# Latent attention in six query tiles: rotated parts of four heads in one tile, score matmuls of 64 and 32 rows for two heads in turn

## The chip, the core and the metric

The kernel runs on one core of a Trainium2 chip (trn2). A core has five engines with queues of their own: PE (TensorE, matrix products), DVE (VectorE), ACT (ScalarE), POOL (GpSimd, which here mostly issues the weight loads) and SP (SyncE, which issues other transfers). Matmuls write to PSUM, eight banks of 128 partitions by 512 fp32 values. The metric is the device time of one execution in microseconds (us), the median of several runs.

## The reference, cut to what matters

The program is two transformer blocks of two layers each, one after the other, over 512 tokens and 1024 features, in fp32. The change concerns one branch of the second block, multi-head latent attention with eight heads:

```
q = (rms_norm(cq, q_norm) @ w_uq).reshape(b, s, 8, 64 + 32)        # cq: 384 wide
q_nope, q_pe = q[..., :64], q[..., 64:]
kv = (rms_norm(ckv, kv_norm) @ w_ukv).reshape(b, s, 8, 64 + 64)    # ckv: 256 wide
k_nope, v = kv[..., :64], kv[..., 64:]
q_pe = apply_rope(q_pe, cos, sin)      # 32 wide, per head
k_pe = apply_rope(kpe, cos, sin)       # 32 wide, one for all heads
sc = (q_nope . k_nope + q_pe . k_pe) * 96 ** -0.5                  # causal mask, softmax, then @ v
```

`apply_rope` turns the two halves of the 32 values: x1 cos - x2 sin and x2 cos + x1 sin. The scores of a head are thus a product over 64 plain features plus one over 32 rotated ones.

## The kernel before

Activations lie feature-major: a tile `s` is 128 features by 512 tokens. Every operand of a large product is kept as a high part h (fp32r) and a rest l, and a product is three matmuls (`mm3`: h.l, l.h, h.h). A weight tile of 128 features by 128 outputs against 512 tokens is thus three matmuls of 128x512.

All work is first recorded as a list of operations (`Plan.record`) and then put in order by a planner (`Plan.schedule`): each engine takes the operation that is due first among those whose inputs it reckons ready and for which a buffer is free (100 `s` tiles of SBUF, 8 `ps` banks). All instructions are issued from one line of `issue`, L649 in the profile (L645 in the changed kernel), so rows are told apart by tile names and shapes. `ps` is a PSUM bank, `s` any SBUF tile, `ident` the identity for transposes.

The second block's layer runs a feed-forward part, the mixer, and another feed-forward part. In the mixer `mla` does the latent attention. It is interleaved with eight pieces of other work (`filler(i)`: two output tiles of the input projection each, 48 matmuls of 128x512, with a recurrent unit or a gated convolution behind them on DVE and ACT), so that PE has something to do while a softmax runs.

In `mla` before, for each head:
- one query tile of 128 rows per head: 64 plain features, the 32 rotated ones and the same 32 with their halves swapped (the columns of w_uq are laid out so). It is 9 matmuls of 128x512 (`pq`); multiplied by one table `self.cs[u]` (ones, cosines, signed sines) it holds what the scores need.
- the key tile has 128 rows to match: 64 rows of k_nope and 64 rows in which the sums that make the rotated key stand twice (`ksum`, `K`; `kk` is filled per pair of heads).
- `attend`: the scores of query block i (128 queries, i = 0 to 3) against the 128(i+1) keys it may see, 3 matmuls over all 128 rows each, into four banks; then `softmax`, then per key block transposes and the product with the values.

The product with the values and `softmax` are the same in both kernels. The first block's attention has scores over 64 rows (`scores` and `ask`): there two heads lie in rows 0 to 63 and 64 to 127 of one tile, and their matmuls are issued in turn.

Of the kernel before, what the change touches and what calls it, by code (L numbers as in the profile page):

```python
# [60 lines left out]
def constants():  # L61
# [25 lines left out]
    for off in (64, 0):  # L87
        r = (p - off) % 128
        is_cos = r < 32
        is_sin = (r >= 32) & (r < 64)  # L90
        cols.append(trig(np.where(r < 64, f2, 0.0), np.where(is_sin, 0.0, 1.0),
                         np.where(is_sin, sg2, 1.0)))
    cols = np.concatenate(cols, 1)
# [57 lines left out]
def lay_out(inp, nl1=2, nl2=2):  # L151
# [37 lines left out]
    uq = []  # L189
    for h in range(8):  # L190
        nope = 96 * h + np.arange(64)
        pe = 96 * h + 64 + np.arange(32)
        uq += [nope, pe, pe[sw]] if h % 2 == 0 else [pe, pe[sw], nope]
    uq = np.concatenate(uq)
# [471 lines left out]
class Net:  # L666
# [230 lines left out]
    def setup(self):  # L897
# [8 lines left out]
        self.cols = self.fixed("cols", [128, 16])  # L906
# [33 lines left out]
    def body(self):  # L940
# [14 lines left out]
        if self.nl2:  # L955
            pf = self.positions(1)
            self.cs = [self.trig(2, pf), self.trig(3, pf)]
# [126 lines left out]
    def attend(self, q, k, rows, rng, nkb, V, vcols, scale, y, yrows, sink=None, mask=None, order=None, starts=(),  # L1084
               stacked=False):
# [3 lines left out]
        lo, hi = rows  # L1089
        S = []  # L1090
        for i in range(4):
            a, b = rng[i]
            w = 128 * (b - a)
            ps = self.ps()[:, :w]
            cols = slice(128 * i, 128 * i + 128)
            kc = slice(128 * a, 128 * b)
            self.mm3(ps, q[0][lo:hi, cols], q[1][lo:hi, cols], k[0][lo:hi, kc], k[1][lo:hi, kc], True, True)
            S.append(ps)
        P = self.softmax(S, scale, sink, mask)
        yield  # L1100
        full = self.ps()
        po = full[0:64]
        order = order or list(range(nkb))
        for n, kb in enumerate(order):
# [8 lines left out]
            if stacked:  # L1113
                mm = nc.tensor.matmul
                mm(full[:, q0:q1], V[kb][:, vcols], h, start=kb in starts, stop=False, skip_group_check=True)
                mm(po[:, q0:q1], V[kb][:, vcols.start:vcols.start + 64], l, start=False, stop=n == nkb - 1,
                   skip_group_check=True)
            else:
                vh, vl = V[0][kb], V[1][kb]
                self.mm3(po[:, q0:q1], vh[:, vcols], vl[:, vcols], h, l, kb in starts, n == nkb - 1,  # L1120
                         skip_group_check=True)
        y = y[yrows[0]:yrows[1]]
        nc.copy(y, po)
        if stacked:
            self.tt(y, full[64:128], ALU.add, out=y)
# [567 lines left out]
    def mla(self, l, z, bias, filler):  # L1693
# [14 lines left out]
        kz = self.stt(z[5][0:64], bias(5)[0:64], self.cs[1][0:64], ALU.add, ALU.mult, out=z[5][0:64])  # L1708
# [6 lines left out]
        K = []  # L1715
        for i in range(4):
            h, l_ = self.t(F32R), self.t(F32R)
            rows = slice(64, 128) if i % 2 == 0 else slice(0, 64)
            self.split(pk[rows], h[rows], l_[rows])
            K.append((h, l_))  # L1720
# [21 lines left out]
        for p in range(4):  # L1742
# [3 lines left out]
            kk = [K[2 * (p % 2)], K[2 * (p % 2) + 1]]  # L1746
            for u in range(2):
                rows = slice(64 * u, 64 * u + 64)
                self.split(ps[rows], kk[u][0][rows], kk[u][1][rows])
            y = self.t()  # L1750
            for u in range(2):
                pq = self.ps()
                wh, wl = self.wsmall(I[f"b_uq{l}"][p][:, 3 * u:3 * u + 3])
                for k in range(3):
                    self.mm3(pq, wh[:, k], wl[:, k], cq[k][0], cq[k][1], k == 0, k == 2)
# [6 lines left out]
                for _ in g:  # L1762
                    pass
# [26 lines left out]
```

## Time and profile before

| | |
|---|---|
| median of 3 runs | 3475.35 us (3474.81 to 3476.16) |
| the profiled execution | 3479.35 us, span of its instructions 3477.6 us |
| PE busy | 3419.1 us, 98% of the span, 16304 matmuls |
| DVE busy | 1916.5 us, 55% |
| ACT, POOL busy | 888.7 us, 1748.9 us |
| granted TensorE clock, mean | 0.992 of full speed |

The span is the time from the first to the last instruction; the execution's own time is 1.75 us longer. Busy time is the union over an engine's instructions. Matmuls overlap in the records (each lasts longer than the distance to the next), so the price of a matmul is the distance between starts, not its own duration.

### The profile page before, as it was taken

The page shows a single profiled execution, that of the slowest core. Times are in us where ns is not written, and L with a number is a line of the kernel's source. Part 1 is how long each engine was busy: PE and PEld are TensorE (multiplying, and loading weights), DVE is VectorE, ACT ScalarE, POOL GpSimd, SP SyncE. Part 2 cuts the span into 40 slices and gives each one's busy share as a digit, 9 for nine tenths or more (in the row PEclk, how much of TensorE's full clock was granted, in tenths as well). Part 3 has the DMA queues.
Part 4 walks back from the last instruction along what each step waited for, and adds up shares of the span by engine and source line. Part 5 has one row for each costly group of instructions (what it writes and reads, how often), then busy time and mean ns, then how long its engine had stood idle before and what let it go on. Part 6 is the DMA issues. An engine that isn't in the chain of part 4 may idle for free.

```text
span 3477.6 us, 44658 instructions
## 1 busy us (share of the span) xinstructions
PE 3419.1 (98%) x16304; PEld 2853.3 (82%) x16304; DVE 1916.5 (55%) x3920; ACT 888.7 (26%) x1723; POOL 1748.9 (50%) x2433
## 2 busy tenths in 40 slices
PE   7999999999999999999999999999999999999998
PEld 5888888788888988888888888888888888888887
DVE  7863424766332733259996534244423999744332
ACT  4740002553000300026723200010001573421000
POOL 3454464354455644653456544654465336654462
PEclk9999999999999999999999999999999999999999
DMA  7788897698789887985899977998899669998794
GB/s 195 150 193 171 163 210 159 134 191 178 156 176 203 207 180 163 236 207 105 174 198 247 216 157 154 222 209 192 159 226 212 126 131 222 231 238 158 158 203 103
DMA packets 360444, 635.93 MB, mean 183 GB/s; under 512 B 40608, under 2 KB 63904, under 8 KB 360224
## 3 DMA queue, kind: packets, MB, share of 16 engines
q0 software_dynamic: 346752, 612.56, 82.7%
q1 hardware_dynamic: 13472, 20.52, 1.9%
q8 instruction: 128, 2.10, 0.2%
q14 instruction: 92, 0.75, 0.1%
HBM read 624.00 MB, written 6.29 MB: 181 GB/s over the span
## 4 chain that ended last, share of the span: by engine, by line
PE 90%; DVE 5%; DMA 2%; issue 1%; ACT 1%; POOL 1%; SPq 0%; DVEq 0%; POOLq 0%; ACTq 0%
PE ps L649 90%; DVE s L649 5%; ACT s L649 1%; DMA s<-in_b_in 1%; DMA s<-in_a_in 1%; POOL s L649 0%; DMA s<-s 0%; SPq L649 0%; DMA s<-in_b_mo 0%; DVE mx L649 0%; DVE sp L649 0%; POOL rinv L649 0%; ACT L649 0%; DVE rc L649 0%; ACT es L649 0%
## 5 line engine op out<-in xcount | busy, mean ns | idle before, releaser
L649 PE MATMUL ps<-s 128*128 128x512 f32 (+4 forms) x15706 | 3363.4, 376 | 42.4 <-DVE s L649 23.7
L649 PEld LDWEIGHTS ps<-s 128*128 128x128 f32 (+2 forms) x15706 | 2780.1, 188 | 592.5 <-ACT s L649 19.2
L649 POOL DMA_DIRECT2D s<-in_b x1088 | 786.4, 1034 | 666.3 <-DVE s L649 307.1
L649 ACT ACTIVATE s<-s 128x512 fp32r<-128x512 f32 (+2 forms) x696 | 393.6, 600 | 1721.1 <-DVE s L649 1133.6
L649 DVE TENSOR_TENSOR s<-ps,s 128x512 f32<-128x512 f32 (+5 forms) x634 | 394.2, 639 | 604.5 <-PE ps L649 601.3
L649 DVE TENSOR_SCALAR s<-s 128x512 fp32r<-128x512 f32 (+2 forms) x851 | 343.7, 423 | 449.7 <-DMA s<-in_b 246.3
L649 POOL DMA_DIRECT2D s<-in_a_f x544 | 397.4, 1037 | 355.0 <-DVE s L649 186.8
L649 DVE TENSOR_TENSOR s<-s 128x512 f32<-128x512 f32 (+3 forms) x812 | 493.0, 625 | 61.9 <-ACT s L649 35.4
L649 POOL DMA_DIRECT2D s<-in_b_in x368 | 290.4, 1017 | 265.5 <-ACT s L649 76.6
L649 DVE SCALAR_TENSOR_TENSOR s<-s,vecs 128x256 fp32r<-128x256 f32 (+22 forms) x438 | 284.1, 684 | 6.4 <-ACT s L649 3.4
L649 ACT ACTIVATE s<-s,vecs 128x512 f32<-128x512 f32 (+2 forms) x209 | 133.8, 661 | 305.6 <-DVE s L649 292.7
L649 DVE SCALAR_TENSOR_TENSOR s<-ps,s 128x512 f32<-128x512 f32 (+1 forms) x33 | 22.3, 675 | 200.0 <-PE ps L649 200.0
L649 ACT ACT_TABLE_LOAD x68 | 87.2, 1283 | 33.3 <-DVE s L649 31.5
L649 ACT ACTIVATE s<-ps 128x512 f32<-128x512 f32 (+1 forms) x40 | 21.4, 534 | 272.8 <-PE ps L649 237.3
L649 POOL DMA_DIRECT2D s<-in_a_in x64 | 47.6, 876 | 83.8 <-ACT s L649 27.4
L649 DVE CAST s<-s 128x512 fp32r<-128x512 f32 (+3 forms) x198 | 83.4, 422 | 5.4
L649 POOL DMA_DIRECT2D s<-in_a_out x64 | 46.5, 1064 | 63.5 <-PE ps L649 23.2
L649 ACT ACTIVATE s<-s,nb 128x256 f32<-128x256 f32 (+3 forms) x128 | 70.7, 555 | 27.1 <-DVE nb L649 27.0
L649 DVE RECIPROCAL s<-s 128x128 f32<-128x128 f32 (+1 forms) x45 | 73.1, 1635 | 7.4 <-ACT s L649 7.4
L649 POOL TENSOR_TENSOR rinv<-rms,nhalf 128x2 f32<-128x2 f32 (+1 forms) x19 | 18.6, 1029 | 98.4 <-DVE rms L649 96.5
L649 POOL DMA_DIRECT2D s<-in_b_out x64 | 48.6, 893 | 34.3 <-DVE s L649 16.2
L649 ACT CAST s<-ps 128x256 fp32r<-128x256 f32 (+4 forms) x131 | 55.9, 464 | 23.7 <-PE ps L649 18.7
(80 smaller groups left out, 905.0 us busy)
## 6 DMA issues: line engine op xcount, KB each, us to landing
s<-in_b POOLq DMA_DIRECT2D x1024, 256.0 KB, 6.4
s<-in_a_f POOLq DMA_DIRECT2D x512, 256.0 KB, 5.9
s<-in_b_in POOLq DMA_DIRECT2D x368, 256.0 KB, 6.3
s<-in_a_in POOLq DMA_DIRECT2D x64, 256.0 KB, 7.6
s<-in_a_out POOLq DMA_DIRECT2D x64, 256.0 KB, 6.5
s<-in_b_out POOLq DMA_DIRECT2D x64, 256.0 KB, 7.4
s<-in_b POOLq DMA_DIRECT2D x64, 128.0 KB, 6.3
s<-in_b_mo POOLq DMA_DIRECT2D x32, 256.0 KB, 6.3
```

Of the source, the lines that this page charges most:

```text
L649: getattr(getattr(nc, op.eng), op.fn)(*[real(v) for v in op.args], **{k: real(v) for k, v in op.kw.items()})
```

## The change

The query features are laid out as eight times 64 plain features (four tiles, one per pair of heads) and then eight times 32 rotated ones (two tiles, four heads each): six tiles, not eight.

```diff
-    uq = []
-    for h in range(8):
...
-        uq += [nope, pe, pe[sw]] if h % 2 == 0 else [pe, pe[sw], nope]
-    uq = np.concatenate(uq)
+    uq = np.concatenate([96 * h + np.arange(64) for h in range(8)] + [96 * h + 64 + np.arange(32) for h in range(8)])
...
-            self.cs = [self.trig(2, pf), self.trig(3, pf)]
+            self.cs = [self.trig(2, pf), self.trig(3, pf), self.trig(4, pf)]
```

The rotated tiles are made at the start of `mla` for all heads. The swap of the halves is done by eight transfers of 16 rows each, issued on SP, from a copy of the PSUM bank:

```diff
+        kp = self.split_t(pk)
...
+        qp = []
+        for t in range(2):
+            ps = query(4 + t)
+            raw, b = self.t(), self.t()
+            nc.copy(raw, ps)
+            for g in range(8):
+                nc.sync.dma_start(out=b[16 * g:16 * g + 16], in_=raw[16 * (g ^ 1):16 * (g ^ 1) + 16])
+            y = self.tt(ps, self.cs[1])
+            self.tt(b, self.cs[2], out=b)
+            qp.append(self.split_t(self.tt(y, b, ALU.add, out=y)))
```

The scores of two heads (u = 0, 1) are made together. For each query block, first the plain part from 64 rows (rows 0 to 63 and 64 to 127), then the rotated part from 32 rows (rows 0 and 32 on, or 64 and 96 on), accumulated in the same bank. A pair holds six banks; blocks 0 and 2 of a head share one.

```diff
+        def scores(p, qn, kn):
+            mm = nc.tensor.matmul
+            banks = [[self.ps() for _ in range(3)] for _ in range(2)]
+            S = [[b[0][:, 0:128], b[1][:, 0:256], b[0][:, 128:512], b[2]] for b in banks]
+            for i in range(4):
+                cols, kc = slice(128 * i, 128 * i + 128), slice(0, 128 * i + 128)
+                for part, (q, k) in enumerate(((qn, kn), (qp[p // 2], kp))):
+                    for n, (x, y) in enumerate(((0, 1), (1, 0), (0, 0))):
+                        for u in range(2):
+                            r = slice(64 * u, 64 * u + 64) if part == 0 else \
+                                slice(32 * (2 * (p % 2) + u), 32 * (2 * (p % 2) + u) + 32)
+                            mm(S[u][i], q[x][r, cols], k[y][r, kc], start=part == 0 and n == 0,
+                               stop=part == 1 and n == 2, skip_group_check=True,
+                               **(dict(tile_position=(r.start, 0)) if part else {}))
+            return S
...
+        heads = pair(0)
+        filler(0)
+        for p in range(4):
+            P = [self.softmax(t, 96 ** -0.5, mask=mask) for t in scores(p, *heads)]
...
+                if h + 1 < 8:
+                    filler(h + 1)
+                if u and p < 3:
+                    heads = pair(p + 1)
+                self.weigh(P[u], rng, 4, V[p // 2], ...)
```

`pair(p)` makes the plain key and query tiles of two heads (6 and 9 matmuls of 128x512, each split once over 128 rows); `weigh` is the second half of `attend`, unchanged.

What this does to the order of instructions is shown at three places. The first is PE in the second block's first layer, the scores of one head before (the second head of the first pair; `ps_14456` to `ps_14463` are its four banks, `s_14448` and `s_14452` its query, the other two its key):

```order
L649 MATMUL ps_14456<-s_14321,s_14448 128x128
L649 MATMUL ps_14458<-s_14321,s_14448 128x256
L649 MATMUL ps_14460<-s_14321,s_14448 128x384
L649 MATMUL ps_14463<-s_14321,s_14448 128x512
L649 MATMUL ps_14456<-s_14308,s_14452 128x128
L649 MATMUL ps_14456<-s_14308,s_14448 128x128
L649 MATMUL ps_14458<-s_14308,s_14452 128x256
L649 MATMUL ps_14458<-s_14308,s_14448 128x256
L649 MATMUL ps_14460<-s_14308,s_14452 128x384
L649 MATMUL ps_14460<-s_14308,s_14448 128x384
L649 MATMUL ps_14463<-s_14308,s_14452 128x512
L649 MATMUL ps_14463<-s_14308,s_14448 128x512
```

These twelve are all of a head's score matmuls, all over 128 rows, and they follow each other. In the changed kernel, PE at the start of the second pair of heads (`ps_14801` and `ps_14803` are the first banks of the two heads; `s_14717` and `s_14711` with `s_14771` and `s_14789` the 64-row parts of keys and queries, `s_14319`, `s_14329` with `s_14458`, `s_14462` the 32-row ones):

```order
L645 MATMUL ps_14801<-s_14717,s_14771 128x128
L645 MATMUL ps_14803<-s_14717,s_14771 128x128
L645 MATMUL ps_14801<-s_14711,s_14789 128x128
L645 MATMUL ps_14803<-s_14711,s_14789 128x128
L645 MATMUL ps_14801<-s_14711,s_14771 128x128
L645 MATMUL ps_14803<-s_14711,s_14771 128x128
L645 MATMUL ps_14801<-s_14329,s_14458 128x128
L645 MATMUL ps_14803<-s_14329,s_14458 128x128
L645 MATMUL ps_14801<-s_14319,s_14462 128x128
L645 MATMUL ps_14803<-s_14319,s_14462 128x128
L645 MATMUL ps_14801<-s_14319,s_14458 128x128
L645 MATMUL ps_14803<-s_14319,s_14458 128x128
```

One query block of two heads is six matmuls of 64 rows and then six of 32 rows, the two heads in turn; the same twelve follow with 256 and 384 columns. The second place is PE at the last query block (512 columns) of that pair, where `ps_14850` and `ps_14865` are the third banks of the two heads and `ps_14759` is a tile of the filler:

```order
L645 MATMUL ps_14850<-s_14717,s_14771 128x512
L645 MATMUL ps_14850<-s_14711,s_14789 128x512
L645 MATMUL ps_14850<-s_14711,s_14771 128x512
L645 MATMUL ps_14850<-s_14329,s_14458 128x512
L645 MATMUL ps_14850<-s_14319,s_14462 128x512
L645 MATMUL ps_14850<-s_14319,s_14458 128x512
L645 MATMUL ps_14759<-s_13575,s_13961 128x512
L645 MATMUL ps_14865<-s_14717,s_14771 128x512
L645 MATMUL ps_14865<-s_14711,s_14789 128x512
L645 MATMUL ps_14865<-s_14711,s_14771 128x512
L645 MATMUL ps_14865<-s_14329,s_14458 128x512
```

Here the two heads do not alternate: the planner found no bank for the second head in time, and its six matmuls come after the first head's six, with a 128-row matmul of the filler between. The third place is SP's queue in the second block's first layer, of the changed kernel:

```order
L645 DMA s<-in_pos 128x512
L645 DMA x<-s 128x512 x8
L645 DMA s<-in_c_ksum 64x128
L645 DMA s<-s 16x512 x16
L645 DMA s<-in_c_mask 128x512
L645 DMA s<-x 128x512 x8
```

The row `s<-s 16x512 x16` is new; before, `s<-in_c_mask` followed `s<-in_c_ksum` at once. It stands once in each of the two layers.

## Rows read from the trace of the kernel before

**Rows 1.** The page: busy time of the engines, granted clock in 40 slices.

```profile
PE 3419.1 (98%) x16304; PEld 2853.3 (82%) x16304; DVE 1916.5 (55%) x3920; ACT 888.7 (26%) x1723; POOL 1748.9 (50%) x2433
PEclk9999999999999999999999999999999999999999
```

**Rows 2.** Windows: feed-forward part, then the latent attention of both layers; columns in the header.

```profile
core 0: us, PE busy (x) PEld busy (x) DVE busy (x) ACT busy (x) POOL busy (x), PEclk, DMA share, GB/s
1200.00:1400.00 200.00, 200.00 (x884) 165.59 (x883) 82.36 (x155) 21.42 (x36) 100.58 (x138) 1.00 0.85 176
1560.00:1740.00 180.00, 177.34 (x860) 145.64 (x859) 171.64 (x373) 126.16 (x236) 72.82 (x102) 1.00 0.68 139
2715.00:2900.00 185.00, 183.18 (x885) 150.31 (x884) 177.53 (x382) 127.44 (x237) 76.98 (x107) 1.00 0.70 141
```

**Rows 3.** Waits of PE in 1560 to 1740: us in total, times, longest.

```profile
PE ps L649 <- DVE s L649: 2.2, 3, 1.5
PE ps L649 <- ACT s L649: 0.4, 1, 0.4
```

**Rows 4.** Timeline of PE: a head's first score matmul, and the matmul after its twelve.

```profile
start us, us, engine line op out<-in xcount [idle before <-releaser]
1583.35 0.22 PE L649 MATMUL ps<-s 128*128 128x128 f32 x1
1585.27 0.39 PE L649 MATMUL ps<-s 128*128 128x512 f32 x1
```

**Rows 5.** Timeline of PE round the first block's 64-row scores (rows*columns of the weights).

```profile
670.25 0.34 PE L649 MATMUL ps<-s 128*64 128x384 f32 x1
670.52 0.39 PE L649 MATMUL ps<-s 64*128 64x256 f32 x2
670.75 0.28 PE L649 MATMUL ps<-s 64*128 64x256 f32 x2
670.98 0.35 PE L649 MATMUL ps<-s 64*128 64x384 f32 x2
...
672.02 0.29 PE L649 MATMUL ps<-s 64*128 64x256 f32 x2
672.25 0.29 PE L649 MATMUL ps<-s 64*128 64x256 f32 x2
672.47 0.50 PE L649 MATMUL ps<-s 128*128 128x512 f32 x1
672.81 0.40 PE L649 MATMUL ps<-s 128*128 128x512 f32 x1
```

**Rows 6.** Groups of PE by shape within that burst, 670.60 to 672.30.

```profile
L649 PE MATMUL ps<-s 64*128 64x384 f32 x12 | 1.2, 332 | 0.0
L649 PE MATMUL ps<-s 64*128 64x256 f32 x12 | 1.1, 293 | 0.0
```

**Rows 7.** Timeline of PE's weight loads at the start of that burst.

```profile
670.52 0.19 PEld L649 LDWEIGHTS ps<-s 64*128 64x128 f32 x2 [0.30 <-issue]
```

**Rows 8.** Groups by shape, whole span: copies and rests of the key halves.

```profile
L649 DVE TENSOR_TENSOR s<-ps,s 64x512 fp32r<-64x512 f32 x24 | 16.5, 686 | 0.5
L649 ACT CAST s<-ps 64x512 fp32r<-64x512 f32 x16 | 9.2, 578 | 5.4 <-DVE s L649 3.1 <-PE ps L649 1.9
L649 DVE CAST s<-ps 64x512 fp32r<-64x512 f32 x8 | 5.5, 688 | 0.2
```

**Rows 9.** SP's transfers from tile to tile: ns per issue (min/median/max), and landing.

```profile
L649 SPq DMA_DIRECT2D s<-s x40: 507/590/832, 28.4 to 635.0; - x40
DMA to landing us min/median/max: 1.9/5.7/11.8
```

**Rows 10.** Windows in the first block: a stretch after PE waited, and one with 64-row scores.

```profile
648.00:654.00 6.00, 0.69 (x3) 0.54 (x3) 5.72 (x18) 1.76 (x6) 0.85 (x1) 0.50 0.22 34
666.00:672.00 6.00, 6.00 (x47) 5.10 (x47) 5.75 (x17) 4.68 (x12) 0.00 (x0) 1.00 0.00 1
```

More of the change, by code (lines that the diff above doesn't have):

```diff
@@ L1082, in softmax, with weigh @@
         return P
-    def attend(self, q, k, rows, rng, nkb, V, vcols, scale, y, yrows, sink=None, mask=None, order=None, starts=(),
-               stacked=False):
+    def weigh(self, P, rng, nkb, V, vcols, y, yrows):
         nc = self.nc
[L1089 to L1100, printed above, removed]
         full = self.ps()
         po = full[0:64]
-        order = order or list(range(nkb))
-        for n, kb in enumerate(order):
+        mm = nc.tensor.matmul
+        for kb in range(nkb):
             qs = [i for i in range(4) if rng[i][0] <= kb < rng[i][1]]
@@ L1112, in attend @@
             self.split(pt, h, l)
[L1113 to L1121, printed above, removed]
+            mm(full[:, q0:q1], V[kb][:, vcols], h, start=kb == 0, stop=False, skip_group_check=True)
+            mm(po[:, q0:q1], V[kb][:, vcols.start:vcols.start + 64], l, start=False, stop=kb == nkb - 1,
+               skip_group_check=True)
         y = y[yrows[0]:yrows[1]]
         nc.copy(y, po)
-        if stacked:
-            self.tt(y, full[64:128], ALU.add, out=y)
+        self.tt(y, full[64:128], ALU.add, out=y)
     def scores(self, heads, rng):
@@ L1714, in mla, with query @@
         nc.tensor.matmul(pk, ksum, kz, start=True, stop=True)
[L1715 to L1720, printed above, removed]
+        kp = self.split_t(pk)
+        qw = {}
+        def query(m):
+            if m // 2 not in qw:
+                qw[m // 2] = self.wload(I[f"b_uq{l}"][m // 2])
+            wh, wl = qw[m // 2]
+            ps = self.ps()
+            for k in range(3):
+                self.mm3(ps, wh[:, 3 * (m % 2) + k], wl[:, 3 * (m % 2) + k], cq[k][0], cq[k][1], k == 0, k == 2)
+            return ps
+        qp = []
[8 more added lines that the diff above has]
+            qp.append(self.split_t(self.tt(y, b, ALU.add, out=y)))
         uv = [self.wsmall(I[f"b_uv{l}"][:, 4 * i:4 * i + 4]) for i in range(2)]
@@ L1741, in mla, with pair @@
         yb = []
-        for p in range(4):
+        def scores(p, qn, kn):
+            mm = nc.tensor.matmul
+            banks = [[self.ps() for _ in range(3)] for _ in range(2)]
[11 more added lines that the diff above has]
+            return S
+        def pair(p):
             ps = self.ps()
```

28 lines of the change are left out of this document (8 added, 20 removed).

## The prediction

> **What bounds the kernel now.** I read the page first, then windows, then waits, then single matmuls. The page has PE busy for 98% of the span at full granted clock [rows 1]; the other engines have slack on the whole. A busy PE could still be a PE that idles in small pieces, so the pace was taken next: in a feed-forward stretch 884 matmuls of 128x512 take 200.00 us, 0.226 us each, and PE never stops [rows 2]. In the stretch where the change acts, latent attention, DVE is the second busiest, 171.64 of 180 us, and PE still runs for 177.34 [rows 2]. All that PE waits for there is 2.6 us in the first layer [rows 3]. So the time of this stretch is the number of PE slots times their price, and work taken from DVE or ACT can give back at most those waits. The sum is a PE sum.
>
> **Queries.** Eight tiles become six: 2 x 9 matmuls of 128x512 fewer in each of two layers, 36 x 0.226 = 8.1 us less. They stand in PE's queue with no wait behind them, so all of it is on the path.
>
> **Scores, if everything ran in pairs.** Before, a head's twelve score matmuls run from 1583.35 to 1585.27, 1.92 us [rows 4]; sixteen heads in two layers are 30.7 us. After, each of these is split in a 64-row and a 32-row one, 384 matmuls for 192. What two such matmuls of different heads cost is read from the first block, where 64-row matmuls of two heads are issued in turn. Each row of the timeline there holds two matmuls, so the two start together; from one such pair to the next, with 256 columns, it is (670.98 - 670.75)/2 = 0.115 us, and with 384 columns (672.02 - 670.98)/6 = 0.173 us [rows 5], for 24 matmuls in all [rows 6]. The pair costs what one matmul costs: 0.173 is 0.226 times 384/512 and a little. Taking the same for 32 rows, two heads need 2 parts x 12 slots where they needed 2 x 12 before: no gain and no loss.
>
> **Scores that have lost their partner.** The order of the changed kernel does not always alternate the heads. A pair wants six banks of eight, and at the last query block the second head often gets its bank too late, so its matmuls come behind the first head's. Over both layers 64 matmuls of 512 columns, 14 of 128 and 2 of 256 have no partner of the same size beside them. Two of these take two slots where a pair takes one: 32 x 0.226 + 7 x 0.12 + 0.12 = 8.2 us more. (A 128-column slot is what is left of a head's 1.92 us: 1.92/3 - 0.226 - 0.173 - 0.115 = 0.126.) This already eats the gain from the queries.
>
> **Changes of row height.** The first block also shows what it costs to go from 128-row to 64-row matmuls. The last of 128 rows starts at 670.25, the first 64-row pair at 670.52, the second at 670.75 [rows 5]: 0.50 us where the slots alone are 0.173 + 0.115 = 0.29. On the way back, 672.25, 672.47, 672.81 [rows 5]: 0.56 where 0.115 + 0.226 = 0.34 were due. So 0.2 us each way. The cause is visible: the weight load, which otherwise runs under the matmul before it, starts only at 670.52, after PE's load port idled for 0.30 us with nothing to wait for but issue, and the matmul has to sit through it (0.39 against 0.28 us) [rows 5, 7]. In the changed order the row height changes 45 times in the first layer's latent attention and 46 times in the second's, against 2 and 2 before (one 64-row product that makes the rotated key): 87 more. 30 of them are between 128 rows and 64 or 32; their price is the one read. The other 57 are between 64 and 32 rows, which nothing in this trace shows. Their bounds are nothing (both are parts of the array, and pairs at rows 0 and 64 do run together [rows 5]) and 0.2 us each. I take 0.2: a 32-row load goes to rows that the 64-row matmul before it is using, as a 64-row load goes to rows that a 128-row one is using, and that is the row that it is nearest to. 87 x 0.197 = 17.1 us.
>
> The Trainium skill, "TensorEngine Tiling (Array Packing)", Key Properties, says the same and against this change: switching the tiling mode, not just the tile, drains the engine. By it all 57 are paid and the sum is as below; without it they would be free and the sum 11.2 us lower. The trace agrees for 128 to 64 rows (0.2 us), and no run so far shows 64 to 32. "TensorE: Matmul & The Clock Gate", Part 3, has matmuls in different row groups run at once, 32-row ones too; the trace agrees for 64 rows.
>
> **What lies beside.** DVE and ACT lose the key halves, 24 copies and 24 rests of about 0.69 us [rows 8]; with the other splits and table products, 28 such DVE operations per layer become 17, 11 x 0.69 = 7.6 us. That is worth at most the 2.6 us of waits [rows 3], and I book nothing, since the new order makes waits of its own that I can't price. If DVE's relief were not there nothing would be lost either. The third table is made once, ahead of feed-forward work in which DVE is busy for less than half [rows 2]. The swap of the rotated halves: a copy, eight issues of 0.59 us, a landing of 5.7 us, then four DVE operations [rows 9, 8]: 0.6 + 4.7 + 5.7 + 2.8 = 13.8 us. In the new order 101 matmuls stand between the end of the query tile and its first use, of which 88 of 512 columns, some 22 us; PE does not wait. DVE waits in order: in its queue the product with the swapped tile stands behind some 39 operations that belong to other work, so it is not early at its wait. SP's queue has the sixteen transfers between two loads that are due later. Uncovered, the swap would cost the 13.8 us once per layer. Weight loads get fewer (twelve query loads per layer for sixteen), on a queue that PE does not wait for.
>
> **The sum.** -8.1 (queries) + 0 (paired scores) + 8.2 (unpaired ones) + 17.1 (row height) = +17.2 us. The profiled execution took 3479.35 us, span 3477.6; it would be 3496.5. It lies 4.0 us over the median of the runs, 3475.35, so the median comes to 3492.5.
>
> **The rivals.** A measurement of this kernel tells a change of 0.2%, 7.0 us, from none; "same" is 3468.4 to 3482.3.
> - *Free inner changes, not slower.* If PE lets a 32-row load run under a 64-row matmul, the 57 cost nothing: -8.1 + 8.2 + 30 x 0.197 = +6.0, 3481.3, inside the 0.2%. It decides from a price under 0.02 us each. For it: two 64-row tiles don't disturb each other [rows 5]. Against: the same rows are in use. 0.10.
> - *Half price.* Drain or load is hidden, not both: 57 x 0.1 less, 3486.8. For it: 0.2 us is two pieces, an idle port and a load [rows 7]. 0.10.
> - *Late swap or new waits.* Landings of 11.8 us [rows 9] and a DVE that is busy for 95% [rows 2] could use up the 8 us of slack; DVE, which works in order, then holds softmax and splits for PE. It costs once the chain passes 22 us, and 6 us per layer would give 3504.5. Against: PE waits for so little now [rows 3]. 0.06.
> - *32-row matmuls don't pair.* Then the rotated part of sixteen heads takes 30.7 us alone where the order's slots are 18.2: +12.5, 3505. For it: no row has 32 rows. 0.04.
> - *The clock.* In a stretch in which PE stood idle for 5.3 of 6 us the granted clock was 0.50, the lower of its two levels (1.2 of 2.4 GHz) [rows 10]; in one with 64-row scores it was 1.00 [rows 10], and the gaps here are 0.2 us. It is in the rest, with a gain that I don't see: 0.03.
>
> **How the numbers follow.** The sum as it stands has 0.67, between 3488 and 3498 (a wait of some us per layer more or less). The rivals have the rest. The likeliest case gives 3492.5. The range from 3481 to 3501 takes in the two cheaper prices of the inner changes and leaves out the late swap, the unpaired 32 rows and the rest, 0.13, with the tails. Faster by over 0.2% would need free changes and pairs where the order has none: 0.02. Within 0.2%: the free inner changes and little else, 0.12. Slower: 0.86.
>
> **What would show it.** In the profile after: groups of 32-row matmuls, two to a start; at each change from 64 to 32 rows a start that comes 0.2 us late, with the load not ahead of its matmul; 512-column score matmuls of one head alone, 0.226 us apart; 18 query matmuls fewer per layer; PE's waits in latent attention still 1 to 5 us. I am wrong if 64 to 32 follows without a gap (then 3481), if one change costs much more than 0.2 us, or if DVE's wait for the swapped tile ends with PE standing still.

## The result and the profile after

The changed kernel takes 3514.76 us, median of four runs (3509.11 to 3520.03), the kernel before 3475.08 in runs beside it (3474.64 to 3476.16): a ratio of 1.011, 95% interval 1.0098 to 1.0123, 39.7 us slower. The prediction was 3492.5, range 3481 to 3501. The sign was right and the size was not: about 22 us are missing in the sum.

The profiled execution took 3520.03 us, span 3518.3. Where the 40.7 us of span lie is found by the matmuls: PE works in program order, so the same matmul of the feed-forward parts can be found in both traces by counting, with 78 more per latent attention in the changed kernel (16460 records for 16304). Before the first latent attention it is 2.6 us later (the variants below are 0.3 to 3.9 us earlier there; nothing was changed in that part, so this is scatter), behind it 24.1, behind the second 41.1. So the first layer's mixer loses 21.5 us, the second's 16.9, and the long feed-forward parts nothing. The page's line of busy times, which answers to [rows 1]:

```profile
PE 3448.2 (98%) x16460; PEld 2860.3 (81%) x16460; DVE 1918.3 (55%) x3923; ACT 860.1 (24%) x1683; POOL 1744.2 (50%) x2425
```

PE is again "busy" for 98%: this number hides all of it. The windows that answer to [rows 2], two of the norm stages, which [rows 2] left out, and the burst (the score matmuls of one pair of heads, one behind the other) of the second pair in four pieces; columns as in [rows 2]:

```profile
1200.00:1400.00 200.00, 200.00 (x884) 165.62 (x883) 84.15 (x160) 22.68 (x37) 97.31 (x134) 1.00 0.84 176
1565.00:1760.00 195.00, 192.09 (x923) 148.73 (x922) 166.38 (x364) 111.72 (x216) 73.00 (x99) 0.95 0.63 130
2745.00:2930.00 185.00, 181.15 (x917) 142.79 (x917) 163.87 (x365) 111.17 (x214) 70.37 (x95) 0.99 0.65 131
...
1547.20:1562.00 14.80, 13.12 (x51) 9.35 (x50) 13.47 (x29) 7.08 (x13) 7.90 (x11) 0.88 0.85 211
2725.10:2742.10 17.00, 12.52 (x48) 8.75 (x48) 13.15 (x27) 6.74 (x13) 8.73 (x13) 0.80 0.91 238
...
1614.00:1620.00 6.00, 6.00 (x39) 4.87 (x38) 5.76 (x13) 4.46 (x9) 2.63 (x3) 1.00 0.63 94
1620.00:1626.00 6.00, 6.00 (x42) 3.53 (x40) 5.87 (x13) 1.19 (x1) 0.84 (x1) 0.88 0.46 75
1626.00:1632.00 6.00, 6.00 (x14) 3.92 (x14) 5.13 (x17) 4.81 (x12) 2.49 (x4) 0.50 0.53 95
1632.00:1638.00 6.00, 6.00 (x22) 4.79 (x21) 2.54 (x8) 1.99 (x5) 0.00 (x0) 0.77 0.30 90
```

The first line agrees with [rows 2] to the matmul. The others show two things that [rows 2] did not have. The granted clock is 0.95 and 0.99 in the scores, where it was 1.00: (1 - 0.95) x 195 + (1 - 0.99) x 185 = 11.6 us. In the burst it falls to 0.50, the lower of its two levels (1.2 of 2.4 GHz), while PE is busy for 6.00 of 6.00 us and never waits; 14 matmuls then take the time of 26. And the norm stages hold few matmuls: 51 records in 14.80 us, 48 in 17.00.

The burst that begins all this is dense only to the eye. Starts of its matmuls, two to a row, which answer to [rows 5]; the last line is the weight load, as in [rows 7]:

```profile
1620.85 0.28 PE L645 MATMUL ps<-s 64*128 64x256 f32 x2
1620.97 0.28 PE L645 MATMUL ps<-s 64*128 64x256 f32 x2
1621.17 0.38 PE L645 MATMUL ps<-s 32*128 32x256 f32 x2
1621.40 0.28 PE L645 MATMUL ps<-s 32*128 32x256 f32 x2
1621.52 0.28 PE L645 MATMUL ps<-s 32*128 32x256 f32 x2
1621.73 0.44 PE L645 MATMUL ps<-s 64*128 64x384 f32 x2
1622.01 0.33 PE L645 MATMUL ps<-s 64*128 64x384 f32 x2
...
1621.17 0.18 PEld L645 LDWEIGHTS ps<-s 32*128 32x128 f32 x2
```

From 64 to 32 rows: 1621.40 - 1620.97 = 0.43 us where two slots of 0.117 were due, 0.20 more. From 32 to 64: 1622.01 - 1621.52 = 0.49 for 0.117 + 0.173, again 0.20. The load starts with its matmul and not ahead of it. Two 32-row matmuls start together, one slot of 0.12 us for both.

The norm stage of the first layer, before and after, as the timeline of PE shows it (idle time in brackets):

```profile
1547.11 0.96 PE L649 MATMUL ps<-ones,s 128*128 128x1 f32 x8
1547.94 2.10 PE L649 MATMUL ps<-s 128*128 128x512 f32 x8
1549.87 0.63 PE L649 MATMUL ps<-s,onesr 128*128 128x512 f32 x2
```

```profile
1549.72 1.05 PE L645 MATMUL ps<-ones,s 128*128 128x1 f32 x8
1552.35 0.80 PE L645 MATMUL ps<-s,onesr 128*128 128x512 f32 x2 [1.58 <-DVE s L645]
1552.95 1.48 PE L645 MATMUL ps<-s 128*128 128x512 f32 x3
1554.46 2.02 PE L645 MATMUL ps<-s,ones 128*128 128x512 f32 x2
1555.55 1.63 PE L645 MATMUL ps<-s 128*128 128x512 f32 x3
```

Before, eight matmuls of the filler stood between the two parts of the norm and covered its chain over DVE. After, nothing stands there, PE waits 1.58 us, and the granted clock of the stretch is 0.88. PE's waits, in the first layer's scores (answers to [rows 3]) and in the two norm stages:

```profile
PE ps L645 <- DVE s L645: 2.9, 6, 0.7
...
PE ps L645 <- DVE s L645: 1.6, 1, 1.6
...
PE ps L645 <- DVE s L645: 4.5, 2, 2.9
```

Before, no wait is listed in either norm stage. So the scores wait little more than before (2.9 us for 2.6 in the first layer, 3.8 for 1.8 in the second), and 6.1 us of waits are new at the norms.

Put together, from start to start over every PE record of the two mixers. A slot is the distance between starts that a shape has at full clock, and a pair has one slot; of a matmul at half clock, what goes beyond its slot is put to the clock; what is left is waits and the rest:

| us, both layers | before | after | difference | predicted |
|---|---|---|---|---|
| slots | 484.3 | 484.3 | 0.0 | +0.1 (-8.1 + 8.2) |
| changes of row height | 1.0 | 17.5 | +16.5 | +17.1 |
| lost to the lower clock | 0 | 12.5 | +12.5 | 0 |
| waits and the rest | 12.2 | 22.1 | +9.9 | 0 |

Of the last two lines 10.3 us lie in the norm stages (3.6 and 6.7, of which 2.2 us are the clock behind the waits) and 10.3 us are the clock in the scores. The four lines come to 38.9 us, where the count of matmuls gave 21.5 + 16.9 = 38.4.

### The profile page after: what moved, and what is told of

Its sections match the earlier page's. It is cut to its first block, busy times and chain, and to the rows that moved or that the text cites. A ratio compares the mean times of both kernels' runs of the same rounds, so it can differ in the third digit from the quotient of the medians.

```text
span 3518.3 us, 44970 instructions
## 1 busy us (share of the span) xinstructions
PE 3448.2 (98%) x16460; PEld 2860.3 (81%) x16460; DVE 1918.3 (55%) x3923; ACT 860.1 (24%) x1683; POOL 1744.2 (50%) x2425
## 4 chain that ended last, share of the span: by engine, by line
PE 88%; DVE 4%; DMA 2%; issue 2%; ACT 1%; POOL 1%; POOLq 0%; DVEq 0%; ACTq 0%
PE ps L645 88%; DVE s L645 4%; ACT s L645 1%; DMA s<-in_b_in 1%; POOL s L645 1%; DMA s<-in_b_uq 0%; DMA s<-in_a_in 0%; DMA s<-in_a_out 0%; DMA s<-in_b_uv 0%; DVE mx L645 0%; ACT L645 0%; POOL rinv L645 0%; DVE rc L645 0%; DVE nb L645 0%; ACT es L645 0%
## 5 line engine op out<-in xcount | busy, mean ns | idle before, releaser
L645 PE MATMUL ps<-s 128*128 128x512 f32 (+6 forms) x15862 | 3385.1, 377 | 48.6 <-DVE s L645 24.5
L645 ACT ACTIVATE s<-s 128x512 fp32r<-128x512 f32 (+3 forms) x662 | 372.6, 598 | 1585.7 <-DVE s L645 1163.4
L645 DVE TENSOR_TENSOR s<-ps,s 128x512 f32<-128x512 f32 (+4 forms) x616 | 381.4, 638 | 583.3 <-PE ps L645 577.0
L645 DVE TENSOR_SCALAR s<-s 128x512 fp32r<-128x512 f32 (+2 forms) x883 | 359.0, 425 | 537.7 <-DMA s<-in_b 317.0
L645 DVE SCALAR_TENSOR_TENSOR s<-s,vecs 128x256 fp32r<-128x256 f32 (+25 forms) x438 | 287.4, 684 | 5.7 <-ACT s L645 1.8
L645 ACT CAST s<-ps 128x512 fp32r<-128x512 f32 (+3 forms) x133 | 56.0, 467 | 32.6 <-PE ps L645 27.9
```

The costliest lines, as they stand in the source:

```text
L645: getattr(getattr(nc, op.eng), op.fn)(*[real(v) for v in op.args], **{k: real(v) for k, v in op.kw.items()})
```

## The experiments

Theory 1, made from this: the rotated query tiles, which stand at the front of the changed `mla`, push the filler out of the norms; and the clock falls in the bursts because PE idles 0.1 us at every change of row height. Its rivals: the norms wait for something else in the new order (theory 2: the filler's weights are queued behind the query weights); the clock falls because of the kind of matmul (theory 2: 32 rows, or one head alone, leave rows of the array unused); the waits come from DVE, which is 95% busy in this stage before the change [rows 2] (theory 3; in the changed kernel it is 85 and 89%, 166.38 of 195 us and 163.87 of 185). Of what the runs gave, "to before" is the difference to the median of the kernel before in runs beside it, "clock" the half-clock loss in the two mixers of the profiled execution, counted as in the table above, and "falls" how often the granted clock fell there inside a burst or right behind it, with no wait of PE in that burst.

| run | row-height changes | median us | ratio (95%) | to before us | clock us | falls |
|---|---|---|---|---|---|---|
| changed kernel | 91 | 3514.8 | 1.011 (1.0098 to 1.0123) | +39.7 | 12.5 | 2 |
| e1_qp_late | 87 | 3523.8 | 1.0132 (1.0118 to 1.0146) | +47.2 | 11.4 | 2 |
| e2_parts | 53 | 3510.7 | 1.0100 (1.0086 to 1.0114) | +34.1 | 10.4 | 3 |
| e5_all64 | 40 | 3509.3 | 1.0088 (1.0074 to 1.0102) | +32.6 | 10.1 | 0 |
| e4_rows128 | 4 | 3484.5 | 1.0024 (1.0015 to 1.0034) | +7.8 | 2.8 | 0 |
| e7_fill | 90 | 3516.8 | 1.0118 (1.0104 to 1.0132) | +42.2 | 10.1 | 3 |
| e9_all64_fill | 42 | 3503.6 | 1.0085 (1.0071 to 1.0099) | +29.0 | 6.7 | 0 |
| e8_rows128_fill | 4 | 3484.1 | 1.0029 (1.0019 to 1.0040) | +9.5 | 0.0 | 0 |
| e10_rows128_split | 4 | 3492.5 | 1.0052 (1.0039 to 1.0065) | +17.9 | 7.6 | 0 |
| n1_before | 4 | 3474.0 | 0.9991 (0.9983 to 1.0000) | -2.9 | 0.0 | 0 |
| n2_after | 87 | 3509.4 | 1.0096 (1.0082 to 1.0109) | +32.5 | 8.5 | 3 |
| n3_rows128_fill | 4 | 3477.7 | 1.0003 (0.9994 to 1.0012) | +0.8 | 1.5 | 0 |
| n4_all64_fill | 36 | 3492.8 | 1.0048 (1.0035 to 1.0060) | +15.9 | 5.6 | 0 |
| e12_rot128 | 80 | 3509.9 | 1.0098 (1.0084 to 1.0112) | +34.1 | 4.4 | 0 |
| n5_after_fill | 86 | 3502.9 | 1.0077 (1.0065 to 1.0090) | +27.1 | 6.0 | 2 |
| e13_rev | 89 | 3516.7 | 1.0113 (1.0097 to 1.0128) | +40.9 | 9.5 | 2 |

### The rotated tiles made later (e1_qp_late)

```diff
-        qp = []
-        for t in range(2):
...
         uk = [self.wsmall(...) for i in range(2)]
+        qp = []
+        for t in range(2):
```

> The two rotated query tiles with their swap are made behind the other loads of mla, no longer ahead of the norms; the scores are those of the changed kernel. By its own order it has 83 row-height changes more than before and some 5.5 us of unpaired slots, so the known terms are -8.1 + 5.5 + 83 x 0.197 = +13.8 us. Theory 1 (the waits of PE at the norms come from the tiles that were moved ahead, the falls of the clock in the score bursts from the row-height changes): the norm waits are back to about 0.8 us per layer, the clock still falls in some score bursts (about 12 us), sum +26, 3501 us, 8 to 14 us under the changed kernel. Rival (the norm waits come from something else in the new order, such as the filler's weights or the key split): still some 10 us there, 3511 us, no clear difference to the changed kernel but for 3 us of fewer changes.

It is 47.2 us slower than before, no faster than the changed kernel and some 13 us above the higher of the two forecasts. At the norms PE waits as before the move; PE's timeline of the first layer there:

```profile
1546.74 1.05 PE L645 MATMUL ps<-ones,s 128*128 128x1 f32 x8
1549.37 0.74 PE L645 MATMUL ps<-s,onesr 128*128 128x512 f32 x2 [1.58 <-DVE s L645]
1549.94 0.86 PE L645 MATMUL ps<-s 128*128 128x512 f32 x3
1553.15 2.07 PE L645 MATMUL ps<-s,ones 128*128 128x512 f32 x2 [2.35 <-DVE s L645]
```

The 1.6 us ahead of the second part of the norm is there in both layers, and ahead of the other norm's sum it waits 2.4 and 3.8 us, where the changed kernel has next to nothing and 2.9. The second layer's scores wait longer too, 8.0 us for DVE where the changed kernel has 2.3. The half of theory 1 that concerns the norms falls.

### All plain parts, then all rotated parts (e2_parts)

```diff
-            for i in range(4):
...
-                for part, (q, k) in enumerate(((qn, kn), (qp[p // 2], kp))):
+            for part, (q, k) in enumerate(((qn, kn), (qp[p // 2], kp))):
+                for i in range(4):
```

> The score matmuls of a pair of heads are issued with all plain parts (64 rows) ahead of all rotated parts (32 rows), so the row height changes 49 times more than before, not 87 times; some 10 us of unpaired slots for 8.2. Known terms: -8.1 + 10 + 49 x 0.197 = +11.6, 5.6 us under those of the changed kernel. Theory 1 (the clock falls because PE idles at each change): the falls inside the bursts go with the changes, the norm waits of some 10 us stay: +22 to +26, 3497 to 3501 us. Rival (matmuls of 32 rows lower the clock whatever stands between them, or the falls come from waits elsewhere): the falls stay, +34, 3509 us.

It is 5.6 us less than the changed kernel against before, what the known terms say, though the intervals of the two ratios overlap. The half-clock loss hardly shrinks (10.4 for 12.5). The burst of the second pair in windows (two stretches ahead of the fall, and the fall), and the groups of the middle one, by shape:

```profile
1614.40:1617.40 3.00, 3.00 (x30) 2.50 (x29) 2.90 (x6) 1.21 (x2) 0.46 (x1) 1.00 0.89 156
1617.40:1620.80 3.40, 3.40 (x27) 2.33 (x25) 3.37 (x5) 0.17 (x1) 0.38 (x1) 1.00 0.48 82
1620.80:1624.20 3.40, 3.40 (x8) 2.14 (x8) 3.39 (x16) 3.37 (x4) 0.83 (x2) 0.50 0.01 2
```

```profile
L645 PE MATMUL ps<-s 64*128 64x512 f32 x6 | 1.9, 422 | 0.0
L645 PE MATMUL ps<-s 32*128 32x512 f32 x3 | 0.9, 390 | 0.0
L645 PE MATMUL ps<-s 32*128 32x384 f32 x6 | 0.7, 332 | 0.0
L645 PE MATMUL ps<-s 32*128 32x256 f32 x6 | 0.6, 293 | 0.0
L645 PE MATMUL ps<-s 32*128 32x128 f32 x6 | 0.6, 288 | 0.0
```

The stretch ahead of the fall has two changes of row height, no wait, and nothing but 32-row pairs and 64- and 32-row matmuls of one head alone. That speaks against the gaps as the cause.

### The rotated part from 64 rows (e5_all64)

```diff
-        kp = self.split_t(pk)
+        kp = [self.split_gain(pk, self.cols[:, 20 + i:21 + i]) for i in range(2)]
...
-                            r = slice(64 * u, 64 * u + 64) if part == 0 else \
-                                slice(32 * (2 * (p % 2) + u), 32 * (2 * (p % 2) + u) + 32)
+                            r = slice(64 * u, 64 * u + 64)
```

The two new columns are one in a head's 32 rows of each 64 and zero in the other's; the rotated heads are laid out in the order 0, 2, 1, 3.

> The rotated part is also made from 64 rows: the other head's 32 rotated rows of the key are set to zero by a column, so that a 64-row matmul gives the same sum. No matmul of 32 rows is left; the row height changes 36 times more than before, all between 128 and 64 rows; some 4.6 us of unpaired slots. Two splits with a gain stand for one split of the rotated key, four rows of 128x512 more per layer on DVE or ACT. Known terms: -8.1 + 4.6 + 36 x 0.197 = +3.6. Theory 1: no fall of the clock in score bursts (at most 3 us), norm waits of some 10 us stay: +14 to +17, 3489 to 3492 us, and the rotated matmuls follow the plain ones without a gap. Rival (64-row scores in dense bursts lower the clock, with or without changes): falls stay, +25, 3500 us.

Both forecasts fail, +14 to +17 and +25: it is +32.6. Every fall of the clock now follows waits of PE of more than 1 us, none begins inside a burst; but there are many such waits, 9.6 us for DVE in the first layer's scores where the changed kernel had 2.9, and they cost about half of what the known terms promised (7.1 us less than the changed kernel, where 17.2 - 3.6 = 13.6 were due).

### 128-row scores from six query tiles (e4_rows128)

From the kernel before: the query tiles of the changed kernel, a plain tile per pair, and for each head

```diff
-                q = self.split_t(self.tt(pq, self.cs[u]))
+                q = self.t(F32R), self.t(F32R)
+                rows, other, src = (slice(64 * v, 64 * v + 64) for v in (u, 1 - u, p % 2))
+                self.split(pq[rows], q[0][rows], q[1][rows])
+                for n in range(2):
+                    nc.copy(q[n][other], qp[p // 2][n][src])
```

> Six query tiles as in the changed kernel, but the scores are those of the kernel before: each head's rotated rows are copied beside its plain rows into tiles of 128 rows (zero rows of the key meet the other head's), and twelve 128-row matmuls per head. No row-height change more than before, nothing unpaired: -8.1 us, known terms. Theory 1 (all that the change loses lies in the row heights, the clock falls that follow them and the moved tiles, which stand late here): 3467 us, faster than before by 0.2%, with PE's waits in latent attention at 2 to 5 us. Rival (the copies and the swap put DVE, 95% busy there, in PE's way): waits of 5 us per layer more, 3477 us, no difference to before.

It is slower by 7.8 us, above both forecasts, where 8.1 us less PE work stands in the program. The row height changes no more often than before here, so another price of "six tiles" is seen: waits of PE in small pieces at scores and transposes, and again the 1.6 us at both norms, though the rotated tiles stand late.

### The filler's first piece recorded first (e7_fill)

```diff
+        filler(0)
         uv = [self.wsmall(...) for i in range(2)]
...
         heads = pair(0)
-        filler(0)
```

> The changed kernel with one line moved: the first filler piece is recorded ahead of the query tiles, so that its weights are due, and loaded, before theirs. By its own order eight filler matmuls stand again between the two parts of the norm, as before. 90 changes of row height, 6.8 us of unpaired slots for 8.2. Theory 2 (the norm waits come from the filler's weights, which are queued behind six-tile query weights, not from where the rotated tiles are made): the waits and the fall of the clock at the norms go, some 10 us; the falls in the score bursts stay, since they come from matmuls that fill a half or a quarter of the array's rows, not from gaps: -8.1 + 6.8 + 86 x 0.197 = 15.6, and some 10 us of clock and waits in the bursts, 3501 us. Rival (the norms wait for their own chain, whatever stands in between): no difference to the changed kernel but for 1.4 us, 3513 us.

The norm of the first layer is as before the change again; PE's timeline there:

```profile
1548.56 0.95 PE L645 MATMUL ps<-ones,s 128*128 128x1 f32 x8
1549.37 2.11 PE L645 MATMUL ps<-s 128*128 128x512 f32 x8
1551.32 0.62 PE L645 MATMUL ps<-s,onesr 128*128 128x512 f32 x2
```

The eight matmuls are back, without a wait and at full clock, in both layers; so the place at which the filler's first piece is recorded was why they had gone. That it is by its weights fits: when the eight would start, 43 of the input projection's loads have landed in the kernel before and in e7_fill, 41 in the changed kernel and 39 in e1_qp_late. The edit moves the piece's matmuls together with its loads, so the weights alone are not shown. (In the second layer 2.2 us of wait ahead of the other norm's sum remain, with a fall of the clock behind them.) But the time is the same as the changed kernel's, within the intervals. The waits in the first layer's scores grew:

```profile
PE ps L645 <- DVE s L645: 7.5, 8, 2.3
```

7.5 us for 2.9, and 5.5 for 3.8 in the second layer: about as much as the norms gave was lost again at the scores. The clock falls inside three bursts, none of them behind a wait.

### The same with 64-row scores (e9_all64_fill)

The edits of e5_all64 and e7_fill together.

> The run before with the rotated part from 64 rows, as in the second-last run of the first batch: 42 changes of row height for 90, 6.9 us of unpaired slots for 6.8, so known terms are 9.4 us less. Theory 2 (32-row matmuls lower the clock): besides the 9.4 us the falls inside bursts that follow no wait are gone; those that follow a wait of PE over 1 us stay; 3486 to 3492 us. Rival (the falls come from waits of PE at softmax and transposes, which this kernel has too): as many half-clock microseconds as in the run before, 3492 to 3498 us.

Against e7_fill 13.2 us less, the 9.4 of the row heights and some 3.4 of clock, as theory 2 has it; the absolute forecast was too low since the waits for DVE are there too:

```profile
PE ps L646 <- DVE s L646: 6.9, 9, 3.2
PE ps L646 <- ACT s L646: 1.1, 2, 1.0
```

All four falls of the clock in this kernel's mixers follow waits of PE that come to 1.3 us or more. (Not every such wait brings a fall: the kernel before waits 1.47 us at 1695.8 without one.)

### Two more with 128-row scores (e8_rows128_fill, e10_rows128_split)

From e4_rows128, with `qp` ahead of the values:

```diff
+        filler(0)
+        qp = []
...
         uv = [self.wsmall(...) for i in range(2)]
...
-                filler(h)
+                if h:
+                    filler(h)
```

> 128-row scores from six query tiles as in the last run of the first batch (+8 us against before, where the sum said -8.1), with the first filler piece and then the rotated tiles recorded ahead of the values, so that the eight filler matmuls stand in the norm again and the swap is early. Theory 2: norm waits back to those of before, -5 us, and no wait of the first scores for the swapped tile, -3 us: 3474 to 3478 us. Rival (the copies of the rotated rows and the splits of 64 rows on a busy DVE are what costs): no gain but the norm's, 3480 us.

The second puts the block that makes one rotated tile in a function, `rotated(t)`:

```diff
-            wh, wl = qw[m // 2]
+            wh, wl = self.wsmall(I[f"b_uq{l}"][m // 2][:, 3 * (m % 2):3 * (m % 2) + 3])
...
+            if p == 2:
+                rotated(1)
             pq = query(p)
```

> As the run before, with the second rotated tile made only ahead of the third pair of heads, and the query weights loaded tile by tile (three blocks of 128 columns, as before the change) and not two tiles at a time. Theory 2 (weights that are loaded before they are needed stand in the way of the filler's): 1 to 4 us less, 3471 to 3475 us, and faster than before if DVE's copies are hidden. Rival: the loads are hidden since the filler is recorded first; no difference to the run before.

Both miss. e8_rows128_fill has no fall of the clock and its first norm without a wait, and is 9.5 us slower than before all the same. Its window in the first layer shows DVE:

```profile
1565.00:1760.00 195.00, 188.63 (x894) 152.75 (x894) 188.03 (x404) 132.38 (x247) 81.32 (x111) 1.00 0.68 144
```

It is 188.03 of 195 us. But in the kernel before DVE is as busy in the same window, with 2.6 us of waits of PE where e8_rows128_fill has 5.7:

```profile
1565.00:1760.00 195.00, 192.34 (x927) 158.26 (x926) 186.00 (x393) 127.58 (x238) 86.37 (x120) 1.00 0.74 152
```

So DVE's busy share alone does not tell the two apart. e10_rows128_split got new waits of 1.6 to 3.3 us, at a norm, at scores and at transposes, and falls of the clock behind them; it is 8.4 us slower than e8_rows128_fill. Why its order is worse was not followed up.

### DVE relieved (n1_before, n2_after, n3_rows128_fill, n4_all64_fill)

One edit in four kernels: the rests of the softmax probabilities are left out and the high part is multiplied in their place, so these kernels return other values and serve for their times alone (in n1_before and n3_rows128_fill `l = h` stands for the last line):

```diff
-            h, l = self.t(F32R)[:, :q1 - q0], self.t(F32R)[:, :q1 - q0]
-            self.split(pt, h, l)
+            h = self.t(F32R)[:, :q1 - q0]
+            nc.copy(h, pt)
...
-            mm(po[:, q0:q1], V[kb][:, vcols.start:vcols.start + 64], l, ...)
+            mm(po[:, q0:q1], V[kb][:, vcols.start:vcols.start + 64], h, ...)
```

> The kernel before without the rests of the softmax probabilities in latent attention: the high part is multiplied twice, and 32 DVE subtractions per layer (1.93 us per head, 15.4 per layer) are left out; PE's matmuls are the same in number and shape. Theory 3 (in latent attention DVE, 95% busy, decides as much as PE; PE's spare time turns into waits for it): PE's waits there shrink a little, 3467 to 3472 us. Rival (PE's own work is the bound, DVE has slack enough): no difference, 3475 us. It is the base for the three that follow.

> The changed kernel without the rests of the probabilities. If DVE's work is behind the waits at the norms and in the scores, what is left against the base is the known sum and the falls of the clock in the bursts: +17 to +26 us. Rival (waits at the norms come from late weights, falls from the kind of matmul, neither from DVE): the same distance as with the rests, +37 to +42 us against the base.

> Six query tiles with 128-row scores and the filler first (+9.5 us against before), without the rests of the probabilities. Theory 3: with DVE relieved, the 36 matmuls saved are seen in the time: -8 us against the base. Rival (the waits come from the order, not from DVE's amount of work): +5 to +9 us against the base, as with the rests.

> Scores from 64 rows alone and the filler first (+29 us against before, where the known terms are +6), without the rests of the probabilities. Theory 3: +6 to +10 us against the base, with no fall of the clock inside a burst. Rival: +25 us or more, with the waits of PE at the first scores of a pair as long as with the rests.

The 64 subtractions, 31 us by the expectation, relieve DVE by less: by the pages its busy time falls by 16 to 25 us in the whole execution (1916.5 to 1898.9 us in the base), and in the scores of n3_rows128_fill it is still 94 and 92% busy. The base gains 2.9 us, with an interval that reaches 1.0000. Against it the others are +35.5 (changed kernel, +39.7 with the rests), +3.7 (n3, +9.5 with them) and +18.9 (n4, +29.0). The forecasts of theory 3 (+17 to +26, -8, +6 to +10) all miss. The relief is worth 10 us to the 64-row variant and 6 to the 128-row one, which still stands 11.8 us above its sum of -8.1; how much of that is DVE's load too is not shown. To the changed kernel it is worth little: there the rival holds. Its scores now wait 2.1 us in the first layer, its norms as long as ever, and its clock falls inside three bursts, none behind a wait.

### The gaps without 32 rows (e12_rot128)

```diff
-        kp = self.split_t(pk)
+        kp = [self.split_gain(pk, self.cols[:, 20 + i:21 + i]) for i in range(4)]
...
-                            r = ... slice(32 * (2 * (p % 2) + u), 32 * (2 * (p % 2) + u) + 32)
+                            r = slice(64 * u, 64 * u + 64) if part == 0 else slice(0, 128)
+                            key = k[y] if part == 0 else k[2 * (p % 2) + u][y]
```

> The changed kernel with the rotated part from all 128 rows of the rotated query tile, against a key that is zero in the rows of the other three heads. The row height still changes in the middle of each pair's scores (80 times in all), but no matmul has 32 rows and the array is full in the rotated part. Each head's rotated part now takes its slots alone: +15.4 us; unpaired slots 3.2 us; 76 x 0.197 = 15.0; with -8.1 the known terms are +25.5, and the norm waits of some 10 us stay. Theory 2 (the clock falls in the bursts where matmuls of 32 rows or of one head leave most of the array's rows unused): no fall inside a burst that no wait of PE over 1 us precedes; 3508 to 3513 us. Rival (the gaps at the changes of row height are what lowers the clock): three or more falls inside bursts, as in the changed kernel; 3517 us or more.

3509.9 us, as theory 2 has it. The burst of the second pair in windows, and its middle by shape:

```profile
1614.00:1618.00 4.00, 4.00 (x33) 3.37 (x32) 3.94 (x7) 0.58 (x1) 0.00 (x0) 1.00 0.00 0
1618.00:1622.00 4.00, 4.00 (x17) 2.48 (x16) 3.94 (x12) 2.77 (x4) 0.04 (x1) 1.00 0.00 0
1622.00:1626.00 4.00, 4.00 (x20) 3.28 (x19) 3.71 (x13) 3.97 (x11) 2.25 (x3) 1.00 0.59 89
```

```profile
L646 PE MATMUL ps<-s 64*128 64x512 f32 x6 | 1.9, 426 | 0.0
L646 PE MATMUL ps<-s 128*128 128x512 f32 x5 | 1.7, 436 | 0.0
L646 PE MATMUL ps<-s 128*128 128x384 f32 x7 | 1.7, 351 | 0.0
L646 PE MATMUL ps<-s 128*128 128x256 f32 x7 | 1.3, 304 | 0.0
```

The order is the same, with the same gaps of 0.1 us at each change, 80 changes for 91: no fall begins inside a burst, where the changed kernel has two. Its three falls come behind waits that come to 1.3 us or more, one of them at a norm. The gaps alone are not the cause.

### The filler first, DVE relieved (n5_after_fill)

The edits of e7_fill and n2_after together.

> The changed kernel without the rests of the probabilities (3509.4 us in the batch before), with the first filler piece recorded ahead of the query tiles. 6.0 us of unpaired slots for 9.1. Theory: the norm's waits come from the filler's late weights, and what moving the filler gives was given back at the scores because DVE was late there; with DVE relieved it is kept: 10 us at the norms and 3 us of slots less, 3496 to 3500 us. Rival (a saved wait at the norms returns at the scores whatever DVE does, since the filler's matmuls are missing there): 3505 us or more.

Against before it is 5.4 us less than n2_after, 3.1 of them slots; the intervals of the ratios overlap a little. The first layer's norms are clean, the second's still wait 3.9 us for DVE ahead of the other norm's sum. So moving the filler is worth some 2 us beyond the slots by the medians, which the overlap leaves unproven; the forecast of 10 was wrong, and the time lies between the two forecasts.

### The widest query block first (e13_rev)

```diff
-            for i in range(4):
+            for i in (3, 2, 1, 0):
```

> The changed kernel with the query blocks of a pair in the order 3, 2, 1, 0: the two heads' matmuls of 512 columns now mostly alternate, the unpaired ones have 256 columns. 4.5 us of unpaired slots for 8.2, 89 changes of row height for 91. By the sum 4 us less than the changed kernel, 3511 us; if unpaired matmuls of 32 and 64 rows are what lowers the clock, some of the falls in the bursts go too, 3503 to 3508 us. Rival: the falls stay as they are, 3511 us.

No gain. Two falls begin inside bursts of the first layer, none in the second; there PE waits 8.5 us for DVE instead of 2.3. Fewer unpaired matmuls alone do not hold the clock up.

## Why the prediction was wrong, step by step

**The PE sum of the scores: right.** Slots came out at 0.0 us where -8.1 + 8.2 stood. 32-row matmuls of two heads run together, so the rival of 32 rows that don't pair falls.

**The row height: right.** The prediction took 0.2 us for a change between 64 and 32 rows, which no row showed; it is 0.20 each way, and 16.5 us in all for 17.1. The rivals of free and of half-priced inner changes fall, and e7_fill against e9_all64_fill agrees (48 changes fewer, 13.2 us, of which 3.4 are clock). The Trainium skill, "TensorEngine Tiling (Array Packing)", Key Properties, says that switching the tiling mode drains the engine; the trace agrees, at 0.20 us.

**The clock: the step that failed, 10.3 us in the scores.** The text gave it 0.03, since "in one with 64-row scores it was 1.00 [rows 10], and the gaps here are 0.2 us". The comparison was with the wrong thing: [rows 10] has no 32-row matmul, and the gaps alone bring no fall (e12_rot128). In seven kernels with 32-row matmuls (the changed one, e1, e2, e7, e13, n2, n5) the granted clock fell inside a burst without a wait of PE 17 times, two or three in each. In those without (e4, e5, e8, e9, e10, e12 and the other n runs) it never did, with the changes of row height (e12) or without. So stretches of 32-row matmuls are what the falls go with. Whether it is the rows that they leave unused or some other trait of them is not shown; 64-row matmuls of one head alone, half the array, are in e9_all64_fill without such a fall. Nor is it shown why only two or three of a kernel's eight bursts have one. The Trainium skill, "TensorE: Matmul & The Clock Gate", Part 1, has the clock follow how busy PE has been; the trace agrees for the falls behind waits (the norm stages at 0.88 and 0.80), and for the 17 others the measurement decides: PE was busy throughout by the profile.

**"I book nothing" for new waits: the other step that failed, 10.3 us.** The rival with waits stood at 0.06, and put them at the swapped tile. The doubt was right and the place wrong: the swap's transfers land in 2.5 us, and the scores wait 2.9 and 3.8 us, inside the 1 to 5 of the prediction. The waits are at the two norms ahead of latent attention, at 1545 to 1557 us before, and the windows that the prediction read begin at 1560 [rows 2, 3]. "Weight loads get fewer (twelve query loads per layer for sixteen), on a queue that PE does not wait for" left the order of the loads out: with the filler's first piece recorded behind the query weights, eight filler matmuls are gone from a gap (e7_fill puts them back), and PE then waits there for DVE's norm chain. Put back, they did not shorten the whole, so the 10.3 us are where the time lies in the changed kernel and not what a mended order would give.

**The premise that PE's work is the time** held for the work added, not for the work taken away. e4_rows128 and e8_rows128_fill take the 8.1 us of query matmuls out, change the row height no more often than before, and end 8 to 9.5 us slower; against a base with the same relief of DVE it is 3.7. DVE stands at 94 to 96% in their scores, and PE's listed waits there are 11.9 us in e8_rows128_fill for 4.4 before. That what PE was spared came back as waits is measured; how much of it is DVE's load and how much the new order is open.

What stays open besides: the wait ahead of the other norm's sum in the second layer (2.2 us in e7_fill, 3.9 in n5_after_fill), and how much of the norms' 10.3 us would be kept in a kernel whose scores do not wait for DVE.

## What to carry to other kernels

Price a small-row matmul by more than its slot: each change of row height cost 0.2 us here, and a stretch of 32-row matmuls can be followed by a lower clock (here for up to 10 us, filler included) without a wait to be seen; read the granted clock of the stretch, not PE's busy share. When code moves ahead in a planned kernel, look at the gaps that its neighbours were filling, the stage ahead too, and at whose weights now come later. Do not book work taken from PE as time saved in a stage where another engine is 95% busy, before a run has shown it.

## What was not expected of the hardware

The granted clock fell to 0.50 with PE busy for 6.00 of 6.00 us, behind stretches of 32-row matmuls, and stayed there for up to 10 us, through matmuls of 128 rows and 512 columns at 0.43 us each where 0.23 is usual. A change between 64 and 32 rows costs as much as one between 128 and 64, 0.20 us at 256 columns and more, in both directions.
